# GpSimd subtractions and products of two tensors in pieces of at most 256 columns, in a two-layer streaming step

## The chip, the core and the metric

The kernel runs on one core of a Trainium2 chip. TensorE (PE in the profile) does the matmuls, VectorE (DVE), ScalarE (ACT) and GpSimd (POOL) work on tiles in SBUF and PSUM, each engine takes its instructions in the order in which they were written to its queue, and semaphores make one engine wait for another. What counts is device time in microseconds, the median over several executions.

## The reference

One step of a two-layer encoder for two request groups: a new stream of 2048 frames with 16 meta tokens ahead of it, and 8 running streams of 16 frames. Together these are 2192 rows of 1024 numbers, all in fp32. Each layer is a norm, one combined input projection, two groups of heads side by side, a gate, and an output projection:

```
layer 0:  u = rmsnorm(x);  p = u @ w_in
          s5_mixer: complex diagonal recurrence, associative_scan over time, gelu, GLU
          mlstm_mixer: xc = silu(causal_conv(x)); q, k = xc @ wq, xc @ wk; v = x @ wv
                       gates = [q k v] @ w_if; chunks of 64 carry (C, n, m)
                       y = head_norm(h) * norm_w + skip * xc
          out = (gated branches) @ w_out, added to x
layer 1:  the same frame with rope, retention (chunked state S), and
rglru_mixer:  xc = causal_conv(x);  r, i = sigmoid(xc @ w_a + b_a), sigmoid(xc @ w_x + b_x)
              a = exp(-8 * softplus(lam) * r);  h_t = a_t * h_(t-1) + sqrt(1 - a_t^2) * (i * xc)
```

The outputs are both groups' rows and every new state. There is no reduced precision: a product of two fp32 tensors is made of rounded halves, as told next.

## The kernel before

An fp32 tensor x that goes into a matmul is cut into two fp32r parts, h = round(x) and l = x - h, and a product is three matmuls (`mm3`, L111 to L113: h*h, l*h or h*l, so that in most places L113 reads the second operand's l and L112 the first one's). `split` (L103) makes the parts: ACT casts x to h at L105, and DVE or, with `pool=True`, GpSimd subtracts at L106. The profile names every split by its tiles: `wl` and `p_wl` are the low parts of weight tiles of 128x1024 (eight blocks of 128 columns), `p_xcl` that of a convolved tile of 128x384 or 128x272, `m_xcl` that of an mLSTM tile of 128x1024, `rol` and `r_gl` those of the last output projection, `p_wal` a 128x256 gate weight.

The stages in the order of time, with the profile's microseconds:

- 0 to 260, input norm and projection of the S5 half of layer 0 (`phase_in0`), weights split on DVE and GpSimd in turn.
- 260 to 900, the other columns of layer 0's projection (`phase_l0`, L341). For every weight tile, projections into `pm`, a causal convolution on DVE (`conv4`, L537 and L539) over `xb`, its split (ACT L389, GpSimd L391 into `xbl`), a SiLU on ACT (L408) and the gate matmuls `pg` (L414) that read its result. Beside it runs the S5 recurrence (`s5`, L676): on DVE a chain of five small instructions per time step (L764 to L768, 0.2 us each).
- 900 to 1230, the mLSTM (`phase_mlstm`, `ml_scores`, `ml_normed`, `ml_gated`), units of 128 rows. GpSimd makes `m_g` = xc * skip (L1161), one step of the normaliser `m_sm` (L1179, L1180), the mask (L1147) and the gate product `m_zb` = m_g * m_zb (L1199); DVE makes `m_qs` (L1131) and adds the normalised heads from PSUM to `m_g` (L1197), which frees the PSUM tile `pa` for the next unit's projection.
- 1230 to 1560, output projection of layer 0.
- 1560 to 2600, input projection of layer 1 (`phase_in1`, L1553). From 1675 it goes in eight periods of 79.2 us, one for each 128 columns of the RG-LRU, with six row blocks b = 0 to 5 each. For a block: PE projects into `p_pm`; ACT copies it to `p_x` (L1612); DVE convolves it into `p_xc` (L537, L539; block 5 also has the running streams, by way of `p_xd`, L1620); ACT casts `p_xch` (L105); GpSimd subtracts `p_xcl` (L106); PE multiplies by the gate weight into `p_pg` (L111 reads `p_xch`, L112 `p_xcl`); ACT and DVE run the gates and the scan (L1632 to L1662, `p_z` last).
- 2600 to 3150, retention and the last output projection (`phase_ret`), whose splits are `r_kl`, `r_pl`, `rol`, `r_gl`, and whose rope product `r_ld` is at L1786.

Tile pools give out buffers and put in the waits. The order within a queue is made by a scheduler that lists the instructions with estimated durations, so a change of some instructions can move others. The order is printed below where it matters.

Of the kernel before, what the change touches and what calls it, by code (L numbers as in the profile page):

```python
# [13 lines left out]
OP = mybir.AluOpType  # L14
# [9 lines left out]
KD = 8  # L24
# [78 lines left out]
def split(nc, h, l, x, pool=False, act=True):  # L103

    (nc.scalar.copy if act else nc.vector.tensor_copy)(h, x)  # L105
    (nc.gpsimd if pool else nc.vector).tensor_tensor(l, x, h, op=OP.subtract)  # L106


def mm3(nc, out, a, b, start, stop, **kw):
# [67 lines left out]
def norm_u(e, ps, x, n, rs, nwb, uh, ul, pname, pbufs, keep=None):  # L177


    nc = e.nc  # L180
    nc.vector.scalar_tensor_tensor(x[:n], x[:n], rs[:n], nwb[:n], op0=OP.mult, op1=OP.mult)
    for g in range(2):
        pt = ps.tile([128, 4, 128], F32, name=pname, bufs=pbufs)
        for j in range(4):
            k = 4 * g + j
            nc.tensor.transpose(pt[:, j, :n], x[:n, 128 * k:128 * (k + 1)], e.ident[:n, :n])
        sl = slice(4 * g, 4 * g + 4)
        split(nc, uh[:, sl, :], ul[:, sl, :], pt[:, :, :n])
        if keep:
            keep(sl, uh[:, sl, :], ul[:, sl, :])  # L190
# [12 lines left out]
def phase_in0(e):  # L203
# [6 lines left out]
    with P(e, "a_w") as wp, P(e, "a_sb", 2) as sb, PS(e, "a_ps") as ps:  # L210
# [37 lines left out]
        for i, bi in enumerate(seq):  # L248
# [8 lines left out]
            if i == 0:  # L257
                m0 = 4
                pms = [ps.tile([128, 384], F32, name="pm0", bufs=4) for _ in range(4)]
                for k in range(KD):  # L260
                    wr = st.tile([128, 1024], F32, name="a_st", bufs=A_ST)
                    nc.sync.dma_start(wr, w[:, k, 0:1024])
                    split(nc, wh[k], wl[k], wr, pool=k % 2 == 1)
                    for m in range(4):
                        mm(pms[m], m, k)
                for m in range(4):
                    out(m, pms[m], zst, b0, n)
# [14 lines left out]
            if i == 4:  # L282

                fp = opn(e, "w_first", side="right")
                wr = sb.tile([128, 1024], F32, name="xt", bufs=3).rearrange("p (k n) -> p k n", n=128)
                nc.sync.dma_start(wr, w[:, :, 1024:1152])
                e.wf = [fp.tile([128, KD, 128], F32R, name="wf" + x) for x in "hl"]
                split(nc, *e.wf, wr)
# [52 lines left out]
def phase_l0(e):  # L341

    nc, tc = e.nc, e.tc
# [12 lines left out]
    def mtile(third, m, isz, ut, pg, parts):  # L356

        h0 = ut[0][1]
        ncol = ut[1][1] + ut[1][2] - h0
# [12 lines left out]
        else:  # L372
            xb = xp.tile([128, 772], F32, name="xb1")
# [14 lines left out]
        xbh = xp.tile([128, 768], F32R, name="xbh1")  # L388
        nc.scalar.copy(xbh[:, :ncol], xb[:, 3:3 + ncol])  # L389
        xbl = xp.tile([128, 768], F32R, name="xbl1")  # L390
        nc.gpsimd.tensor_tensor(xbl[:, :ncol], xb[:, 3:3 + ncol], xbh[:, :ncol], op=OP.subtract)  # L391
        xc = sb.tile([128, 768], F32, name="xc1")
        if third == 0:
            nc.gpsimd.memset(xb[:, 0:3], 0.0)
# [63 lines left out]
    for third in range(3):  # L458
# [6 lines left out]
        if third > 0:  # L465

            early = [mtile(third, 0, 0, ut, pg, parts),
                     mtile(third, third % 2 == 0, third % 2, ut, pg, parts)]
            for g in early:
                next(g)  # L470
            reload(2 * third + 1)
            e.s5.loaded = third == 2
# [576 lines left out]
def ml_scores(e, sb, lp, hp, pt, slots):  # L1049


    nc, v = e.nc, e.nc.vector
    sk = e.row["ml_skip"]
    dec, meta = slots[0] == 0, slots[0] == 1
    n = NM if meta else 128
# [24 lines left out]
    if meta:  # L1080

        for g in range(2):
            pq = pt("pa", 2, 256)
            for j in range(2):
                for k in range(2):
                    c = 4 * g + 2 * j + k
# [8 lines left out]
    for g in range(0 if meta else 4):  # L1095
        pq = pt("pa", 2, N)
        for j in range(2):
            ms = slice(128 * j, 128 * (j + 1))
            for k in range(2):
                c = 2 * g + k  # L1100
# [6 lines left out]
        if dec:  # L1107
            pk = pt("pa", 2, N)
            for j in range(2):
                for k in range(2):  # L1110
                    c = 2 * g + k
# [4 lines left out]
    for i, slot in enumerate(slots):  # L1116
        r0, cc, cs = H * slot, c0 + n * i, slice(n * i, n * (i + 1))
        c = Env()
# [17 lines left out]
        for g in range(2):  # L1136
# [3 lines left out]
            for j in range(2):  # L1140
                h = 2 * g + j
# [16 lines left out]
        p = c.p = sb.tile([128, H, 128], F32, name="m_p", bufs=nb(2))  # L1158
        v.tensor_tensor(p[:n, :, :n], pS[:n, :, :n], w[:n, :, :n], op=OP.mult)
        g = c.g = sb.tile([128, KD, 128], F32, name="m_kt" if dec else "m_g", bufs=nb(2))  # L1160
        nc.gpsimd.tensor_tensor(g[:, :, :n], c.xc, e.pc[:, :, sk:sk + 1].to_broadcast([128, KD, n]), op=OP.mult)  # L1161
        res.append(c)
    return res

# [19 lines left out]
def ml_gated(e, c):  # L1184

    nc, v = e.nc, e.nc.vector
    nw, g, n = e.row["ml_norm_w"], c.g, c.n
    zb = c.sb.tile([128, KD, 128], F32, name="m_rw" if c.dec else "m_zb", bufs=1 if c.dec else 2)
    nc.sync.dma_start(zb[:, :, :n], e.zb[:, :, c.c0:c.c0 + n])
    for q in range(2):  # L1190
        py = c.pt("pa", 4, 128)
        for j in range(4):
            k = 4 * q + j
            nc.tensor.transpose(py[:, j, :n], c.yn[:n, k // 2, 128 * (k % 2):128 * (k % 2 + 1)], e.ident[:n, :n])
        for j in range(4):
            k = 4 * q + j
            v.scalar_tensor_tensor(g[:, k, :n], py[:, j, :n], e.pc[:, k, nw:nw + 1], g[:, k, :n],  # L1197
                                   op0=OP.mult, op1=OP.add)
    nc.gpsimd.tensor_tensor(zb[:, :, :n], g[:, :, :n], zb[:, :, :n], op=OP.mult)  # L1199
    nc.scalar.dma_start(e.gb[:, :, c.c0:c.c0 + n], zb[:, :, :n])  # L1200


def ml_running(e, sb, pt):


    nc, v, m = e.nc, e.nc.vector, e.m
    c, = ml_scores(e, sb, sb, sb, pt, [0])
    z = sb.tile([128, 2, NSEQ, 2 * LS], F32, name="m_z")
    nc.gpsimd.memset(z, 0.0)
# [846 lines left out]
```

## Time and profile before

| what | us |
|---|---|
| median of 3 runs | 3155.74 (3153.85 to 3159.35) |
| the profiled execution | 3151.14 |
| its span, first to last instruction | 3149.4 |
| PE busy | 3002.9 (95%), 17435 matmuls |
| DVE busy | 1728.6 (55%) |
| ACT busy | 1056.1 (34%) |
| GpSimd busy | 904.6 (29%), 931 instructions |

"Busy" is the time from an instruction's start to its end as the profiler records it, so an instruction that has started and cannot get at its data counts as busy. The mean granted clock of PE is 0.980. Between the first matmul and the last, PE stands still in some 77 gaps, about 130 us in all.

### The profile page before, as it was taken

To read this page: it belongs to the slowest core of one execution; us is meant where nothing else is said; L and a number is where in the kernel's file an instruction comes from. 1 tells how busy PE (TensorE), PEld (TensorE's weight loads), DVE (VectorE), ACT (ScalarE), POOL (GpSimd) and SP (SyncE) were. 2 spreads that over 40 slices of the span, in tenths; PEclk is the share of its full clock that TensorE was granted. 3 is DMA by queue.
4 is the path that set the end of the run, shared out by engine and by line. 5 is a ranking of instruction groups with operands and counts; after the bars stand their busy time and mean duration, and the time that the engine had idled before them with its cause. 6 is when DMAs were issued, how large, how long until landed. Compare 5 with 4: busy or idle time off the path is not lost.

```text
span 3149.4 us, 45106 instructions
## 1 busy us (share of the span) xinstructions
PE 3002.9 (95%) x17435; PEld 2717.0 (86%) x17435; DVE 1728.6 (55%) x3449; ACT 1056.1 (34%) x1858; POOL 904.6 (29%) x931
## 2 busy tenths in 40 slices
PE   8999978997999998999999999999999999999999
PEld 8999877996987887766799999999998897888887
DVE  4236798464447886243355667766620026665664
ACT  4223332335334443211224555555531112211211
POOL 6104424443225663111202111111110014433432
PEclk9999989998999999999999999999999999999999
DMA  6437433559454556755532111111122158444442
GB/s 213 117 82 206 125 117 113 159 166 177 141 159 125 157 156 183 232 185 172 158 132 73 51 51 50 49 50 49 49 81 75 55 151 251 140 119 133 136 124 74
DMA packets 444034, 396.36 MB, mean 126 GB/s; under 512 B 43401, under 2 KB 392785, under 8 KB 443818
## 3 DMA queue, kind: packets, MB, share of 16 engines
q1 hardware_dynamic: 333164, 268.13, 29.9%
q10 hardware_dynamic: 110654, 125.33, 12.0%
q8 instruction: 137, 2.24, 0.3%
q14 instruction: 79, 0.65, 0.1%
HBM read 262.12 MB, written 131.27 MB: 125 GB/s over the span
## 4 chain that ended last, share of the span: by engine, by line
PE 59%; DVE 8%; DMA 2%; issue 1%; ACT 1%; POOL 0%; SPq 0%; DVEq 0%; POOLq 0%; ACTq 0%
PE p_pm L112 8%; PE p_pm L113 8%; PE p_pm L111 8%; PE r_pm L112 4%; PE r_pm L113 4%; PE r_pm L111 4%; PE pa L111 3%; PE pa L112 3%; PE pa L113 3%; DVE p_d L1639 1%; PE pn L1288 1%; PE pc L1291 1%; DVE p_xc L537 1%; PE pa L1156 1%; DVE m_qs L1131 1%
## 5 line engine op out<-in xcount | busy, mean ns | idle before, releaser
L111 PE MATMUL p_pm<-pu,p_wh 128*128 128x384 f32 (+1 forms) x1568 | 512.2, 327 | 0.2 <-ACT pu L105 0.2
L112 PE MATMUL p_pm<-pu,p_wh 128*128 128x384 f32 (+1 forms) x1568 | 511.9, 327 | 0.0
L113 PE MATMUL p_pm<-pu,p_wl 128*128 128x384 f32 (+1 forms) x1568 | 511.3, 326 | 0.0
L111 PE MATMUL pm<-ub,wh 128*128 128x384 f32 (+1 forms) x1136 | 381.4, 336 | 3.4 <-ACT wh L105 2.9
L112 PE MATMUL pm<-ub,wh 128*128 128x384 f32 (+1 forms) x1136 | 380.1, 335 | 1.6 <-DVE ub L106 1.6
L113 PE MATMUL pm<-ub,wl 128*128 128x384 f32 (+1 forms) x1136 | 376.1, 334 | 0.0
L111 PEld LDWEIGHTS p_pm<-pu,p_wh 128*128 128x128 f32 x1568 | 294.2, 188 | 1.8 <-issue 1.2
L112 PEld LDWEIGHTS p_pm<-pu,p_wh 128*128 128x128 f32 x1568 | 294.6, 188 | 1.0 <-issue 0.8
L113 PEld LDWEIGHTS p_pm<-pu,p_wl 128*128 128x128 f32 x1568 | 294.5, 188 | 0.0
L111 PEld LDWEIGHTS pm<-ub,wh 128*128 128x128 f32 x1136 | 218.6, 193 | 9.0 <-issue 4.3
L112 PEld LDWEIGHTS pm<-ub,wh 128*128 128x128 f32 x1136 | 218.7, 193 | 3.0 <-DVE ub L106 2.1
L112 PE MATMUL r_pm<-rol,r_gh 128*128 128x512 f32 x544 | 217.6, 400 | 3.8 <-POOL rol L106 3.6
L113 PEld LDWEIGHTS pm<-ub,wl 128*128 128x128 f32 x1136 | 218.1, 192 | 1.2 <-issue 1.1
L111 PE MATMUL r_pm<-roh,r_gh 128*128 128x512 f32 x544 | 217.5, 400 | 0.9 <-ACT p_o L1549 0.9
L113 PE MATMUL r_pm<-roh,r_gl 128*128 128x512 f32 x544 | 216.9, 400 | 0.9 <-DVE r_gl L106 0.9
L106 POOL TENSOR_TENSOR p_wl<-p_wr,p_wh 128x1024 fp32r<-128x1024 f32 x34 | 81.8, 2407 | 385.3 <-ACT p_wh L105 372.9
L106 POOL TENSOR_TENSOR wl<-wr,wh 128x1024 fp32r<-128x1024 f32 x47 | 119.2, 2537 | 243.1 <-ACT wh L105 236.8
L112 PEld LDWEIGHTS r_pm<-rol,r_gh 128*128 128x128 f32 x544 | 102.7, 189 | 24.3 <-POOL rol L106 4.1
L113 PEld LDWEIGHTS r_pm<-roh,r_gl 128*128 128x128 f32 x544 | 102.8, 189 | 22.6 <-DVE r_gl L106 1.3
L111 PEld LDWEIGHTS r_pm<-roh,r_gh 128*128 128x128 f32 x544 | 102.3, 188 | 21.9 <-ACT p_o L1549 1.3
L106 POOL TENSOR_TENSOR p_xcl<-p_xc,p_xch 128x384 fp32r<-128x384 f32 (+1 forms) x48 | 46.8, 975 | 245.9 <-ACT p_xch L105 209.3
L1639 DVE RECIPROCAL p_d<-p_d 128x384 f32<-128x384 f32 (+1 forms) x48 | 116.7, 2430 | 0.6
(715 smaller groups left out, 6810.9 us busy)
## 6 DMA issues: line engine op xcount, KB each, us to landing
wr<-in_ev_w_in_dram SPq DMA_DIRECT2D x47, 512.0 KB
p_wr<-in_od_w_in_dram SPq DMA_DIRECT2D x40, 512.0 KB
d_in<-p_o ACTq DMA_DIRECT2D x80, 192.0 KB
m_rw<-d_grow SPq DMA_DIRECT2D x18, 512.0 KB
s5u<-d_ua SPq DMA_DIRECT2D x32, 274.0 KB
d_v<-vo ACTq DMA_DIRECT2D x68, 128.0 KB
m_va<-d_v SPq DMA_DIRECT2D x17, 512.0 KB
d_h<-o_x ACTq DMA_DIRECT2D x17, 512.0 KB
```

The lines of the kernel that those rows point to most:

```text
L106: (nc.gpsimd if pool else nc.vector).tensor_tensor(l, x, h, op=OP.subtract)
L111: nc.tensor.matmul(out, a[0], b[0], start=start, stop=False, **kw)
L112: nc.tensor.matmul(out, a[0], b[1], start=False, stop=False, **kw)
L113: nc.tensor.matmul(out, a[1], b[0], start=False, stop=stop, **kw)
L537: v.tensor_scalar(out, x(3), pc[:, m, cw + 3:cw + 4], pc[:, m, cb:cb + 1], op0=OP.mult, op1=OP.add)
L1131: v.tensor_tensor(qs[:, 4 * j:4 * j + 4, :n].rearrange("p (h m) n -> p h m n", m=2), qt[j][:, :, cs].rearrange("p (h m) n -> p h m n", m=2 ...
L1156: nc.tensor.matmul(pS[:n, h, :n], ktc[:, 2 * h + k, :], qt[h // 2][:, 2 * (h % 2) + k, cs], start=k == 0, stop=k == 1)
L1288: nc.tensor.matmul(pn[:n], c.qs[:, 2 * h + k, :n], ct[h][:, k, :], start=False, stop=k == 1)
L1291: nc.tensor.matmul(pc, c.kw[:n, h, 128 * k:128 * (k + 1)], c.va[:n, h, :], start=True, stop=True)
L1639: v.reciprocal(d[:, :n], d[:, :n])
```

## The change

A helper `narrow` issues a GpSimd `tensor_tensor` as several over slices of the first free dimension, such that none has more than 256 columns per partition. It takes the place of the single instruction in `split(pool=True)`, for `xbl`, for `m_g` (L1161) and for `m_zb` (L1199). All else is left: the rope product (L1786), the S5 products (L753, L818), and the splits on DVE. Line numbers after the helper grow by 12 (L111 becomes L123).

```diff
 def split(nc, h, l, x, pool=False, act=True):
     (nc.scalar.copy if act else nc.vector.tensor_copy)(h, x)
-    (nc.gpsimd if pool else nc.vector).tensor_tensor(l, x, h, op=OP.subtract)
+    if pool:
+        narrow(nc, l, x, h, OP.subtract)
+    else:
+        nc.vector.tensor_tensor(l, x, h, op=OP.subtract)
+
+def narrow(nc, out, a, b, op):
+    n = out.shape[1]
+    step = max(1, 256 * n // math.prod(out.shape[1:]))
+    for i in range(0, n, step):
+        c = slice(i, min(i + step, n))
+        nc.gpsimd.tensor_tensor(out[:, c], a[:, c], b[:, c], op=op)
...
-        nc.gpsimd.tensor_tensor(xbl[:, :ncol], xb[:, 3:3 + ncol], xbh[:, :ncol], op=OP.subtract)
+        narrow(nc, xbl[:, :ncol], xb[:, 3:3 + ncol], xbh[:, :ncol], OP.subtract)
...
-        nc.gpsimd.tensor_tensor(g[:, :, :n], c.xc, e.pc[:, :, sk:sk + 1].to_broadcast([128, KD, n]), op=OP.mult)
+        narrow(nc, g[:, :, :n], c.xc, e.pc[:, :, sk:sk + 1].to_broadcast([128, KD, n]), OP.mult)
...
-    nc.gpsimd.tensor_tensor(zb[:, :, :n], g[:, :, :n], zb[:, :, :n], op=OP.mult)
+    narrow(nc, zb[:, :, :n], g[:, :, :n], zb[:, :, :n], OP.mult)
```

The program's GpSimd instructions grow from 936 to 1589, those of the other engines stay the same but for three table loads of ACT fewer. The order moves too.

GpSimd in the mLSTM, around the gate product of one unit; before:

```order
L1199 TENSOR_TENSOR m_zb_10464<-m_g_9963,m_zb_10464 128x1024
L1147 AFFINE_SELECT m_w_10360<-m_w_10360 128x512
L1179 TENSOR_TENSOR m_sm_10805<-m_sm_10805,mhalf_84 128x1
L1161 TENSOR_TENSOR m_g_10335<-m_xc_10227,pc_549 128x1024
L1180 TENSOR_SCALAR m_sm_10805<-m_sm_10805 128x1
L1199 TENSOR_TENSOR m_zb_10571<-m_g_10005,m_zb_10571 128x1024
```

and the same unit after:

```order
L118 TENSOR_TENSOR m_zb_10391<-m_g_9866,m_zb_10391 128x256 x4
L1159 AFFINE_SELECT m_w_10284<-m_w_10284 128x512
L118 TENSOR_TENSOR m_g_10256<-m_xc_10142,pc_561 128x256 x4
L1191 TENSOR_TENSOR m_sm_10708<-m_sm_10708,mhalf_84 128x1
L118 TENSOR_TENSOR m_zb_10501<-m_g_9911,m_zb_10501 128x256
L1192 TENSOR_SCALAR m_sm_10708<-m_sm_10708 128x1
L118 TENSOR_TENSOR m_zb_10501<-m_g_9911,m_zb_10501 128x256 x3
```

One row has become four instructions, `m_g` goes ahead of a step of the normaliser, and such a step now stands between two pieces.

PE in `phase_in1`, where the first gate matmul of block 5 (`p_pg` from `p_xch`) stands in the next projection (`p_pm`, tile by tile of `pu`); before:

```order
L111 MATMUL p_pm_16174<-pu1_14739,p_wh_16142 128x384
L112 MATMUL p_pm_16174<-pu1_14739,p_wh_16142 128x384
L113 MATMUL p_pm_16174<-pu1_14739,p_wl_16143 128x384
L111 MATMUL p_pm_16174<-pu1_14739,p_wh_16142 128x384
L111 MATMUL p_pg_16081<-p_xch_16077,p_wah_15586 128x384
L112 MATMUL p_pm_16174<-pu1_14739,p_wh_16142 128x384
```

and after, ahead of these rows the first four matmuls of the same tile:

```order
L124 MATMUL p_pm_16596<-pu1_15146,p_wh_16561 128x384
L125 MATMUL p_pm_16596<-pu1_15146,p_wl_16562 128x384
L123 MATMUL p_pm_16596<-pu1_15146,p_wh_16561 128x384
L124 MATMUL p_pm_16596<-pu1_15146,p_wh_16561 128x384
L125 MATMUL p_pm_16596<-pu1_15146,p_wl_16562 128x384
L123 MATMUL p_pm_16596<-pu1_15146,p_wh_16561 128x384
L124 MATMUL p_pm_16596<-pu1_15146,p_wh_16561 128x384
L125 MATMUL p_pm_16596<-pu1_15146,p_wl_16562 128x384
L123 MATMUL p_pm_16596<-pu1_15146,p_wh_16561 128x384
L123 MATMUL p_pg_16500<-p_xch_16495,p_wah_15999 128x384
L123 MATMUL p_pg_16506<-p_xch_16495,p_wah_15999 128x384
```

The gate matmul stands nine matmuls of 128x384 later in that tile. DVE in the same place, from the end of block 4's scan to block 5's convolution; before:

```order
L1609 MEMSET p_x_17101 128x3
L1662 TENSOR_TENSOR p_z_16685<-p_z_16685,p_h_16658 128x384
L537 TENSOR_SCALAR p_xc_16806<-p_x_16803,pc_549 128x256
L1620 COPY p_xd_16811<-p_x_16803 128x8x16
L1622 COPY p_cs_14751<-p_x_16803 128x3
L539 SCALAR_TENSOR_TENSOR p_xc_16806<-p_x_16803,pc_549,p_xc_16806 128x256
L537 TENSOR_SCALAR p_xc_16806<-p_xd_16811,pc_549 128x128
```

and after:

```order
L549 TENSOR_SCALAR p_xc_17239<-p_x_17236,pc_561 128x256
L1632 COPY p_xd_17244<-p_x_17236 128x8x16
L1634 COPY p_cs_15158<-p_x_17236 128x3
L1674 TENSOR_TENSOR p_z_17117<-p_z_17117,p_h_17090 128x384
L551 SCALAR_TENSOR_TENSOR p_xc_17239<-p_x_17236,pc_561,p_xc_17239 128x256
L549 TENSOR_SCALAR p_xc_17239<-p_xd_17244,pc_561 128x128
```

The convolution now begins ahead of `p_z`.

## Rows read from the trace of the kernel before

**Rows 1.** The page's first part: engine, busy us (share of the span), instructions.

```profile
PE 3002.9 (95%) x17435; PEld 2717.0 (86%) x17435; DVE 1728.6 (55%) x3449; ACT 1056.1 (34%) x1858; POOL 904.6 (29%) x931
```

**Rows 2.** Waits of PE: what waited, for whom, total us, times, longest.

```profile
PE pg L414 <- ACT xc L408: 29.9, 9, 6.7
PE pa L111 <- DVE m_g L1197: 17.3, 5, 3.5
PE p_pg L111 <- ACT p_xch L105: 10.6, 8, 1.4
...
PE r_pm L112 <- POOL rol L106: 3.6, 1, 3.6
```

**Rows 3.** Groups by shape, POOL: busy us, mean ns, idle before and releasers.

```profile
L106 POOL TENSOR_TENSOR p_wl<-p_wr,p_wh 128x1024 fp32r<-128x1024 f32 x34 | 81.8, 2407 | 385.3 <-ACT p_wh L105 372.9 <-DMA p_wr<-in_od_w_in_dram 12.4
...
L106 POOL TENSOR_TENSOR p_wal<-p_wax,p_wah 128x256 fp32r<-128x256 f32 x8 | 5.9, 737 | 64.2 <-ACT p_wah L105 64.2
```

**Rows 4.** Timeline, DVE, S5 recurrence at 395: start, us, instruction.

```profile
395.70 2.42 DVE L768 TENSOR_TENSOR s5ee<-s5c,s5c 128x32 f32<-128x32 f32 x1
398.15 1.24 DVE L764 TENSOR_TENSOR s5c<-s5ee,s5a 64x32 f32<-64x32 f32 x1
399.41 0.21 DVE L765 TENSOR_TENSOR s5c<-s5ee,s5a 64x32 f32<-64x32 f32 x1
```

**Rows 5.** Timeline, POOL, the same stretch.

```profile
395.64 2.40 POOL L106 TENSOR_TENSOR wl<-wr,wh 128x1024 fp32r<-128x1024 f32 x1 [2.30 <-ACT wh L105]
398.00 1.35 POOL L391 TENSOR_TENSOR xbl<-xb,xbh 128x656 fp32r<-128x656 f32 x1
```

**Rows 6.** Timeline, all engines, the mLSTM unit at 1164.

```profile
1164.12 2.35 POOL L1199 TENSOR_TENSOR m_zb<-m_g,m_zb 128x1024 f32<-128x1024 f32 x1 [3.01 <-DMA m_rw<-d_grow]
...
1164.35 3.71 DVE L1131 TENSOR_TENSOR m_qs<-m_qt,m_rw 128x512 f32<-128x512 f32 x2
...
1166.43 1.09 POOL L1147 TENSOR_SCALAR_AFFINE_SELECT m_w<-m_w 128x512 f32<-128x512 f32 x1
...
1168.11 1.11 DVE L1197 SCALAR_TENSOR_TENSOR m_g<-pa,pc,m_g 128x128 f32<-128x128 f32 x4
...
1169.28 0.58 PE L111 MATMUL pa<-m_xch,amh 128*128 128x256 f32 x1 [3.46 <-DVE m_g L1197]
```

**Rows 7.** Timeline, DVE: another `m_qs` pair, then a period of `phase_in1`.

```profile
1184.96 1.29 DVE L1131 TENSOR_TENSOR m_qs<-m_qt,m_rw 128x512 f32<-128x512 f32 x2 [1.83 <-DMA m_rw<-d_grow]
...
1796.25 0.49 DVE L1662 TENSOR_TENSOR p_z<-p_z,p_h 128x384 f32<-128x384 f32 x1
...
1800.49 2.58 DVE L1662 TENSOR_TENSOR p_z<-p_z,p_h 128x384 f32<-128x384 f32 x1
...
1804.62 2.53 DVE L537 TENSOR_SCALAR p_xc<-p_xd,pc 128x128 f32<-128x128 f32 x1
...
1808.21 0.72 DVE L539 SCALAR_TENSOR_TENSOR p_xc<-p_xd,pc,p_xc 128x128 f32<-128x128 f32 x2
```

**Rows 8.** Timeline, POOL, the same period.

```profile
1800.26 2.39 POOL L106 TENSOR_TENSOR p_wl<-p_wr,p_wh 128x1024 fp32r<-128x1024 f32 x1 [13.72 <-ACT p_wh L105]
1802.91 1.03 POOL L106 TENSOR_TENSOR p_xcl<-p_xc,p_xch 128x384 fp32r<-128x384 f32 x1 [0.26 <-ACT p_xch L105]
1804.65 2.41 POOL L106 TENSOR_TENSOR p_wl<-p_wr,p_wh 128x1024 fp32r<-128x1024 f32 x1 [0.71 <-ACT p_wh L105]
```

**Rows 9.** Timeline, ACT and PE, the same period.

```profile
1801.88 0.48 ACT L1612 COPY p_x<-p_pm 128x384 f32<-128x384 f32 x1
...
1809.58 0.44 PE L111 MATMUL p_pg<-p_xch,p_wah 128*128 128x384 f32 x1 [1.40 <-ACT p_xch L105]
```

**Rows 10.** Timeline, DVE and POOL, the convolution at 360 in `phase_l0`.

```profile
358.90 3.33 POOL L106 TENSOR_TENSOR wl<-wr,wh 128x1024 fp32r<-128x1024 f32 x1
...
359.94 2.98 DVE L539 SCALAR_TENSOR_TENSOR xc<-xb,pc,xc 128x656 f32<-128x656 f32 x1
```

**Rows 11.** Timeline, POOL, the retention stage at 2669, behind the rope product.

```profile
2669.82 2.34 POOL L106 TENSOR_TENSOR rol<-r_yn,roh 128x1024 fp32r<-128x1024 f32 x1
```

## The prediction

> **What bounds the kernel now.** The page first: PE is busy 95% of the span, DVE 55%, POOL 29% [rows 1]. GpSimd has some 2245 us in which nothing runs, so its own busy time sets no bound. PE's gaps come to about 130 us, and nothing off PE can give back more than that. So the second view is who PE waits for [rows 2]. Two large entries name DVE as the last link: the gate matmuls `pg`, which wait for ACT's SiLU, itself fed by DVE's convolution (29.9 us), and the mLSTM projection `pa`, held by DVE's `m_g` (17.3 us in five waits). A third, `p_pg` (10.6 us in eight), waits for ACT's cast of what DVE convolved. Only 3.6 us name POOL.
>
> The third view is DVE beside POOL. In the S5 recurrence a DVE instruction of 32 columns lasts 0.21 us. The one that starts at 395.70, just after GpSimd's `wl` split (395.64, 2.40 long), lasts 2.42, to 398.12; the next, under `xbl` (398.00, 1.35), lasts 1.24 and ends at 399.39 [rows 4, 5]. A DVE instruction with its data in SBUF stands still until the GpSimd instruction that runs has ended; then DVE gets one instruction in, and the next GpSimd instruction blocks it again. It repeats: `p_z` lasts 2.58 at 1800.49 under `p_wl` and 0.49 at 1796.25 alone; one `p_xc` of 128 columns lasts 2.53 under the next `p_wl` [rows 7, 8]; two `m_qs` take 3.71 under `m_zb` and the mask, and 1.29 without [rows 6, 7]. The price also runs the other way: `wl` at 358.90 takes 3.33, nearly 1 us above its usual length [rows 10].
>
> The Trainium skill ("SBUF — State Buffer", "Who interferes with whom") says the same: VectorE's second port pair is GpSimd's, and it is an exclusive lock for a whole instruction. The durations just named agree.
>
> So the question is whether a lock held for about 0.65 us, four times, costs the path of PE's gaps less than one held for 2.4.
>
> **The change part by part.** GpSimd's own time: a 128x256 subtraction takes 0.737 us, one of 1024 columns 2.407 [rows 3]. Four are 2.948, so 0.541 more, or 180 ns for each instruction added. 653 more instructions make up to 118 us of POOL time, less some 40 ns each for the overlap that two instructions in a row show (395.64 + 2.40 against 398.00): 91 to 118 us. Off the path this costs nothing: the weight splits run a projection tile ahead of their use, and POOL idles over twice a microsecond for each one added. If that cover were gone, PE would wait for `wl`, `p_xcl` or `rol`; that is a rival below. A piece's data part is 0.737 - 0.180 = 0.56.
>
> Where a single DVE instruction meets a long split, it waits for one piece instead of the whole:
>
> - The convolution at 360: L539 of 656 columns lasts 2.98, about 0.9 of it work. With GpSimd's pieces of 0.65 to 0.74 its wait falls from about 2.1 to 0.7: **-1.35** in a PE gap of 3.38 that waits for `pg`. The same gap of the second pass, at 673, has 3.11 us and a similar chain: **-1**. Bounds together 0 (the following convolution steps meet the pieces left over) to -3.
> - The mLSTM: five gaps of 3.46 us, alike. In the last, `m_zb` runs from 1164.12, the mask behind it, and the two `m_qs` between end at about 1168.0; `m_g` follows at 1168.11 and PE at 1169.28 [rows 6]. After the change the queue there still has `m_zb`, then the mask. The first `m_qs` waits for one piece (to about 1164.8) and ends at 1165.35, the second for the next piece (to 1165.95) and ends at 1166.5, L1178 for the third; `m_g` begins at about 1167.2 instead of 1168.1. That is -0.9 each, **-4.5**. Bounds: 0, if the pieces hold DVE as long as before, to five times -1.3. The normaliser step that now stands behind `m_g`'s four pieces comes 2 us later; its reader on ACT ran at 1172.7, with PE's transposes of it a unit behind, so that is cover enough.
> - `phase_in1`, eight gaps of 1.40 at `p_pg` of block 5 [rows 2, 9]. Two things change. DVE: the convolution starts ahead of `p_z`, and ACT's copy `p_x` no longer stands behind a table load, so that it follows the weight cast at once (`p_wl`, which waits for that cast, starts at 1800.26 [rows 8]) and is there at about 1800.7 instead of 1802.36 [rows 9]. The chain (two L537, six L539, three copies and `p_z`, about 3.9 us of work) now lies under two `p_wl` of eight pieces: four from 1800.2, four from 1804.65, when the second cast has come. Nearly every one of its instructions waits for a piece: 1800.7 + 3.9 + about 4.3 = 1808.9, the same end as before (1808.93, [rows 7]). DVE as such gains nothing here. PE: the gate matmul stands nine matmuls of 0.174 us later, 1.57 us that used to be gap and now is work. 1.40 - 1.57 is below nothing, so about 1.2 of each gap goes: **-9** over eight. Bounds: -11 (all) to +3 (the chain 0.7 later than PE's new arrival plus the 1.40). Block 4 comes to its gate matmul 1 us earlier, but its convolution is done by 1799 and the matmul is due at about 1802.7.
> - The retention gap of 3.64 us [rows 2]: `rol` starts at 2669.82 behind the rope product and takes 2.34 [rows 11]; PE reads it block by block, so it can go on after the first pieces: **-0.9**, bounds 0 and -1.6.
>
> Where DVE is dense with small instructions (S5 recurrence, 380 to 510), the lock alternates: seven pieces in place of `wl` and `xbl` block seven instructions for a short time instead of two for a long one. Before, DVE lost 2.42 + 1.24 - 2 x 0.22 = 3.2 us [rows 4]. After, the data parts hold it just as long (3.2), and the five fixed parts of 180 ns hold it fully or not at all: 3.2 to 4.1. Some 38 added instructions in that stretch make 0 to +7 us on DVE. The chain that ends `pg`'s 23 us of gaps there runs over DVE, but most of its convolution steps meet no split. I take **0**, with -2 to +7.
>
> The rest is order: the stretch 900 to 1230 and the gaps at 745 to 785, which an ACT instruction behind a DMA sets, come in another order on all engines. I see no sign to give them: **0**, with 6 either way.
>
> Sum: -2.3 - 4.5 - 9 - 0.9 = -16.7 us. The profiled execution took 3151.1, 4.6 below the median of the runs, so 3134 in a profile and **3139 us** as a median, -0.5%. Shorter gaps may also spare some stretches at the lower granted clock that follow the long ones; I count nothing for it.
>
> **Rivals.**
> *The alternation takes it all back (no change).* If after each piece DVE gets exactly one instruction, every dense chain loses what it lost. Then the mLSTM and convolution terms fall to about nothing and the dense stretch pays +4, while PE's reorder in `phase_in1` gives half: about 3155. For it speak the two blocked instructions in a row at 395.70 and 398.15; against it that the mLSTM's pair is only two instructions long.
>
> *The fixed part decides (slower).* Each piece costs DVE its whole 0.737, not 0.56: +7 in the S5 stretch; in `phase_in1` eight pieces add 8 x 0.18 = 1.4 to the chain, which gives the 1.2 back; in the mLSTM units 12 pieces for `m_zb`, `m_g` and `m_xcl` add some 9 x 0.18 = 1.6 each, in about eight units before their gap ends, 8 to 13 us. Sum about +10 to +18: 3168. It decides if DVE loses over 0.65 us for each piece it meets. The Trainium skill ("GPSIMD Engine Reference", section 3.1 and the dispatch figures beside it) has a fixed cost for each GpSimd instruction, which speaks for such a price; the 180 ns above are this kernel's.
>
> *POOL comes late (slower).* Between two pieces DVE takes its turn, so a four-piece split lasts up to 4 x (0.74 + 0.5) = 5 us beside a dense DVE. `p_xcl` in two pieces ends some 0.4 us later; the time between PE's L111 and L112 that hides it is 1.04 us where it is least, and `p_xcl` alone takes 1.03 [rows 8]. If PE waits 0.5 us at each of the 48, that is +24 against -17: 3163.
>
> *More is won.* If `pg`'s gaps of 5 to 7 us also shrink by a piece's difference, and lower-clock stretches go with them: another -12, 3127.
>
> **How the numbers follow.** Forecast as summed 0.50, more won 0.13, alternation 0.20, the two slower ones 0.17 together. A measurement of this kernel can tell 0.2% (6.3 us) from no change: faster, below 3149.4, takes the first two and a little of the third: 0.66. Same, to 3162: 0.19. Slower 0.15. The range reaches from "more won" with its reorder bound (3121) to the slower cases' lower part (3162); the forecast's own range is 3129 to 3149.
>
> **What would show it.** In the profile after: a 128x256 row of `wl` at about 0.65 to 0.74 us and POOL at about 1000 us busy; no DVE row of 2.4 us under a split, but runs of several at 0.6 to 0.8; PE's five waits for `m_g` at about 2.6 us; the eight waits for `p_xch` gone or below 0.3; no wait of PE for POOL's `p_xcl`. I am wrong if the S5 stretch's `pg` waits grow by more than a few us, or if new waits come up in the mLSTM.

## The result and the profile after

The change makes the kernel slower: median 3169.48 us (3165.16 to 3172.07, five runs) against 3153.85 (3149.38 to 3159.35, five runs) for the kernel before, a ratio of 1.0054 with the interval [1.0041, 1.0068]. The forecast, 3139, had the wrong sign, and the time lies 7.5 us above the range.

The page's first part of the changed kernel (engine, busy us, share of the span, instructions; span 3167.8 us), against [rows 1]:

```profile
PE 3013.3 (95%) x17435; PEld 2719.1 (86%) x17435; DVE 1663.7 (53%) x3449; ACT 1051.8 (33%) x1855; POOL 1093.3 (35%) x1584
```

DVE is 65 us less busy: as meant, it stands less behind GpSimd. Yet PE is 10.4 us busier with the same matmuls (10.3 of it in the retention stage, where the mean granted clock is 0.97 instead of 0.99), and it stands still longer by the rest of the 18.4 us that the span has grown. To see where, the span is cut at the same six matmuls in both traces. The busy time by stage (window, its length, then busy us and instructions of PE, PEld, DVE, ACT, POOL, then PE's granted clock, DMA share, GB/s), kernel before:

```profile
0.00:913.00 913.00, 827.77 (x5369) 793.23 (x5369) 515.79 (x918) 321.28 (x605) 324.25 (x292) 0.96 0.53 149
913.00:1220.00 307.00, 275.35 (x1608) 239.12 (x1609) 241.44 (x716) 127.47 (x269) 172.48 (x208) 0.93 0.48 144
...
1682.00:2287.00 605.00, 594.38 (x3570) 591.83 (x3569) 425.81 (x709) 323.62 (x495) 103.82 (x76) 1.00 0.15 48
...
2643.00:3149.00 506.00, 493.35 (x2481) 411.66 (x2479) 305.59 (x621) 101.51 (x158) 192.04 (x184) 0.99 0.45 129
```

The same stages of the changed kernel:

```profile
0.00:907.00 907.00, 823.16 (x5369) 788.04 (x5369) 488.67 (x918) 320.43 (x603) 414.42 (x539) 0.97 0.52 150
907.00:1230.00 323.00, 279.51 (x1614) 237.21 (x1615) 215.93 (x724) 125.89 (x271) 192.12 (x344) 0.94 0.46 138
...
1693.00:2284.00 591.00, 591.00 (x3562) 591.00 (x3561) 428.26 (x707) 323.76 (x491) 138.52 (x188) 1.00 0.15 50
...
2644.00:3168.00 524.00, 503.61 (x2483) 418.71 (x2481) 297.08 (x624) 101.04 (x158) 223.32 (x277) 0.97 0.44 125
```

Two stages gain: everything up to 913 us by 6, and `phase_in1` by 14, where PE now never stops (591.00 of 591.00). Two lose more: the mLSTM (907 to 1230) takes 16 us longer, though DVE is 25.5 us less busy there, and the retention stage 18. PE's idle time grows from 31.7 to 43.5 us in the mLSTM and from 12.7 to 20.4 in the retention stage.

Who PE waits for (what waited, for whom, total us, times, longest), the answer to [rows 2]:

```profile
PE pg L426 <- ACT xc L420: 27.0, 10, 5.9
PE pn L1298 <- ACT m_yn L1193: 15.1, 5, 5.5
PE pc L1303 <- DVE ct L1307: 14.8, 8, 4.9
...
PE pa L1206 <- ACT m_yn L1193: 6.5, 4, 3.4
PE r_pm L125 <- DVE r_gl L109: 6.0, 2, 4.2
...
PE r_pm L123 <- ACT roh L105: 3.1, 1, 3.1
PE pa L123 <- DVE m_g L1209: 3.0, 2, 1.5
...
PE r_pm L124 <- POOL rol L118: 0.9, 3, 0.5
```

What was to shrink has shrunk: `pa` for `m_g` from 17.3 to 3.0, `rol` from 3.6 to 0.9, `p_pg` for `p_xch` from 10.6 to no entry at all. But `pn` and `pa` for ACT's `m_yn`, `pc` for `ct` (4.4 us in the mLSTM before) and `r_pm` for `r_gl` and `roh` are new or much larger.

GpSimd's groups by shape (busy us, mean ns, idle before), against [rows 3]:

```profile
L118 POOL TENSOR_TENSOR wl<-wr,wh 128x256 fp32r<-128x256 f32 x188 | 179.1, 983 | 180.0 <-ACT wh L105 179.8
L118 POOL TENSOR_TENSOR p_wl<-p_wr,p_wh 128x256 fp32r<-128x256 f32 x128 | 103.3, 838 | 253.2 <-ACT p_wh L105 253.2
```

On the mean a piece of these splits lasts 0.84 to 0.98 us, not the 0.737 of [rows 3]. The mean hides two kinds (shortest, median and longest in ns):

```profile
L118 POOL TENSOR_TENSOR wl<-wr,wh x188: 719/741/2615, 255.0 to 892.7; 128x256 fp32r<-128x256 f32 x188
```

Half of the pieces take 0.741 us or less, beside the small DVE instructions of S5 too (four in 2.82 us, below); each of the 51 that take over 1 us overlaps a DVE instruction of 512 columns or more (convolutions, S5 products). The stretch of S5 that [rows 4, 5] showed, on DVE and then on GpSimd (start, us, instruction):

```profile
390.30 0.73 DVE L777 TENSOR_TENSOR s5c<-s5ee,s5a 64x32 f32<-64x32 f32 x1
391.06 0.67 DVE L778 TENSOR_TENSOR s5c<-s5ee,s5a 128x32 f32<-128x32 f32 x1
391.65 0.80 DVE L779 TENSOR_TENSOR s5c<-s5c,s5ee 128x32 f32<-128x32 f32 x1
392.48 0.66 DVE L780 TENSOR_TENSOR s5ee<-s5c,s5c 128x32 f32<-128x32 f32 x1
393.18 0.54 DVE L776 TENSOR_TENSOR s5c<-s5ee,s5a 64x32 f32<-64x32 f32 x1
393.73 0.58 DVE L777 TENSOR_TENSOR s5c<-s5ee,s5a 64x32 f32<-64x32 f32 x1
```

```profile
390.24 2.82 POOL L118 TENSOR_TENSOR wl<-wr,wh 128x256 fp32r<-128x256 f32 x4 [3.77 <-ACT wh L105]
393.03 1.63 POOL L118 TENSOR_TENSOR xbl<-xb,xbh 128x256 fp32r<-128x256 f32 x3
```

One DVE instruction passes per piece (one more, not shown, runs under the end of the seventh and last piece, in 0.37 us). The six come to 3.98 us where 6 x 0.22 = 1.32 would do: 2.7 lost, against the 3.2 of before. The Trainium skill ("SBUF — State Buffer", "Who interferes with whom") calls the shared port pair an exclusive lock; the trace agrees, with 0.54 to 0.80 us for each of the six instructions shown.

### The profile page after: what moved, and what is told of

It reads as the page before. It is cut to its first block, busy times and chain, and to the rows that moved or that the text cites. A ratio compares the mean times of both kernels' runs of the same rounds, so it can differ in the third digit from the quotient of the medians.

```text
span 3167.8 us, 45858 instructions
## 1 busy us (share of the span) xinstructions
PE 3013.3 (95%) x17435; PEld 2719.1 (86%) x17435; DVE 1663.7 (53%) x3449; ACT 1051.8 (33%) x1855; POOL 1093.3 (35%) x1584
## 4 chain that ended last, share of the span: by engine, by line
PE 77%; DMA 8%; DVE 8%; POOL 3%; issue 2%; ACT 1%; ACTq 1%; SPq 0%; DVEq 0%; POOLq 0%
PE p_pm L125 10%; PE p_pm L124 10%; PE p_pm L123 10%; PE r_pm L125 4%; PE r_pm L124 4%; PE r_pm L123 4%; PE pm L123 4%; PE pm L124 4%; PE pm L125 4%; PE pa L123 3%; PE pa L124 3%; PE pa L125 3%; DMA m_rw<-d_grow 2%; DVE xc L551 1%; PE pn L1300 1%
## 5 line engine op out<-in xcount | busy, mean ns | idle before, releaser
L123 PE MATMUL p_pm<-pu,p_wh 128*128 128x384 f32 (+1 forms) x1568 | 512.5, 327 | 0.2 <-ACT pu L105 0.2
L123 PE MATMUL pm<-ub,wh 128*128 128x384 f32 (+1 forms) x1136 | 380.3, 336 | 10.0 <-ACT vo L451 8.8
L123 PEld LDWEIGHTS p_pm<-pu,p_wh 128*128 128x128 f32 x1568 | 294.5, 188 | 1.4 <-issue 0.8
L118 POOL TENSOR_TENSOR wl<-wr,wh 128x256 fp32r<-128x256 f32 x188 | 179.1, 983 | 180.0 <-ACT wh L105 179.8
L123 PEld LDWEIGHTS pm<-ub,wh 128*128 128x128 f32 x1136 | 217.4, 192 | 15.0 <-ACT vo L451 9.4
L123 PE MATMUL r_pm<-roh,r_gh 128*128 128x512 f32 x544 | 220.0, 405 | 3.3 <-ACT roh L105 3.1
L118 POOL TENSOR_TENSOR p_wl<-p_wr,p_wh 128x256 fp32r<-128x256 f32 x132 | 108.4, 852 | 262.0 <-ACT p_wh L105 262.0
L118 POOL TENSOR_TENSOR p_xcl<-p_xc,p_xch 128x256 fp32r<-128x256 f32 x96 | 61.4, 660 | 319.6 <-ACT p_xch L105 284.4
L123 PEld LDWEIGHTS r_pm<-roh,r_gh 128*128 128x128 f32 x544 | 104.4, 192 | 25.2 <-ACT roh L105 3.3
```

Of the source, the lines that this page charges most:

```text
L118: nc.gpsimd.tensor_tensor(out[:, c], a[:, c], b[:, c], op=op)
L123: nc.tensor.matmul(out, a[0], b[0], start=start, stop=False, **kw)
```

## The experiments

**Theories.** *Order* (mine, after seeing the traces): the pieces do what the forecast says, but with 653 more instructions the scheduler lists all queues in another order, and that order is worse in the mLSTM and the retention stage. *Pieces*: their fixed cost and the alternation with DVE are the loss. To part them, the order of a queue has to be set apart from the pieces. An order table does it: every instruction is tied to the one that is to stand ahead of it on its queue, by an edge that fixes the order and adds no semaphore. The table itself costs nothing that can be seen: e9 below holds the change's own order by one, and its time isn't told apart from the change's.

```diff
+def pinned(tc):
...
+        for p, q in zip(row, row[1:]):
+            tc.add_manual_dep(own[q], own[p].name, dep, reason="order")
...
+        pinned(tc)
```

In e1 the changed kernel has the order of before on all queues (the pieces where the whole stood). In e2 the kernel before has the order of after (a whole instruction where its last piece stands).

> The changed kernel's pieces, with every engine's queue in the order of the kernel before (a piece stands where its whole instruction stood). Theory 'order': the loss of the change (+19 us in the retention stage, +12 in the mLSTM, by the time between the same matmuls in the two traces) comes from the new order, and the pieces themselves help: some 3140 to 3150 us, ratio 0.995 to 0.999, with the five waits for m_g at about 2.6 us and no wait of PE for m_yn. The eight waits of p_pg stay near 1.4 to 1.6 us, since their gain was PE's order. Theory 'pieces': what is lost is DVE and GpSimd time under the lock, so the loss stays without the new order: 3163 us or more, ratio 1.003 or more.

> Whole GpSimd instructions as before, with every engine's queue in the order of the changed kernel (a whole instruction stands where its last piece stood). Theory 'order': as slow as the changed kernel or slower, 3165 to 3180 us, ratio 1.004 to 1.009, with the long waits for m_yn in the mLSTM. Theory 'pieces': no loss, 3145 to 3157 us, ratio 0.997 to 1.001, with the eight waits of p_pg shorter.

| | whole | pieces of 256 |
|---|---|---|
| order of before | 1 | e1: 0.9954 [0.9938, 0.9969], 3134.75 us |
| order of after | e2: 1.0143 [1.0128, 1.0159], 3195.25 us | 1.0054 [1.0041, 1.0068] |

The pieces gain in either order, 0.5% in the old and 0.9% in the new one. The order costs 1.4% with whole instructions and 1.0% with pieces. So *pieces* falls as the cause of the loss; e2's loss is even larger than *order* expected (1.009 at most). The waits of PE in e1:

```profile
PE pg L428 <- ACT xc L422: 22.5, 10, 4.7
PE pa L1170 <- DVE m_p L1173: 10.7, 6, 2.2
...
PE p_pg L125 <- ACT p_xch L107: 9.8, 7, 1.4
...
PE pa L125 <- DVE m_g L1211: 7.8, 5, 1.8
```

The five waits for `m_g` fall from 3.46 to 1.6 us each, and those for `p_xch` stay, as the forecast's steps say. But six waits for `m_p`, 10.7 us, are new, and in the mLSTM they take the place of what `m_g` gives back. The stage's window in e1:

```profile
908.00:1206.00 298.00, 266.98 (x1607) 230.37 (x1608) 230.89 (x721) 127.94 (x271) 200.16 (x342) 0.97 0.50 149
```

PE stands still for 31.0 us there, against 31.7 before. What the stage gains is PE's busy time, 275.35 to 266.98, with a granted clock of 0.97 instead of 0.93: the gaps are shorter and more, and by these means PE spends some 18 us at the lower of its clock levels instead of 43.

**Where.** The difference to the trace of before by stage, between the same matmuls (us; one execution each, whose time lies up to 6 us from the median of its kernel, e13's 6.0 below it; a stage with the same queues and instructions differs by up to 5 us between two executions, as e4 with -3.4 and e5 with +1.7 do up to 913; mLSTM to the last `pn` from `ct`, then to the first `p_pg`, the last `p_pg`, the last `p_pm`, the end):

| | to 913 | mLSTM | to 1682 | in1 | to 2643 | retention | all |
|---|---|---|---|---|---|---|---|
| after | -5.8 | +15.6 | +1.7 | -14.4 | +3.7 | +17.5 | +18.3 |
| e1 pieces, old order | -4.5 | -9.2 | +1.7 | -1.1 | +0.5 | +0.4 | -12.2 |
| e2 whole, new order | +0.1 | +31.6 | -1.5 | -6.5 | +1.3 | +18.2 | +43.2 |
| e8 mixed order | -10.8 | -7.7 | +2.3 | -12.6 | +2.2 | +1.0 | -25.6 |
| e10 old load queue | -2.5 | +1.0 | +20.3 | -14.0 | +8.0 | +17.6 | +30.4 |
| e13 the same, to mLSTM's end | -11.7 | +4.0 | +1.5 | -14.4 | +1.7 | +17.0 | -1.9 |

The retention stage loses about the same with whole instructions (+18.2) as with pieces (+17.5): nothing but order is left there. In `phase_in1` order and pieces share the gain: the eight waits come to 10.6 before, 9.8 with pieces alone, 5.7 with the order alone, and none with both.

**One stage at a time, scheduler free.** The step becomes the whole tile outside the named stages.

```diff
-    step = max(1, 256 * n // math.prod(out.shape[1:]))
+    step = max(1, 256 * n // math.prod(out.shape[1:])) if STAGE[0] in PIECES else n
...
+PIECES = ('phase_in0', 'phase_l0', 'phase_in1')
```

e4 has `('phase_mlstm',)` there and e5 `('phase_ret',)`.

> Pieces in the two input projections (phase_in0, phase_l0, phase_in1) alone, whole instructions elsewhere; the scheduler then leaves the queues of the mLSTM, the output projection and the retention stage as they were before. By the time between the same matmuls in the two traces these stages gave -12 (to 760 us), +6 (760 to 900) and -13 (1680 to 2360). Theory 'order' and theory 'pieces' both: 3132 to 3140 us, ratio 0.993 to 0.996, if the loss of the other stages is their own; near 3154 if it was passed on from the earlier stages.

> Pieces in the mLSTM (phase_mlstm) alone; other stages' queues as before. If the mLSTM's own new order makes its loss: +8 to +18 us, 3162 to 3172, ratio 1.003 to 1.006, with PE waiting for m_yn. If the loss there came from what the earlier stages shifted: -4.5 us as I summed, ratio 0.998 to 1.000.

> Pieces in the retention stage (phase_ret) alone, whole instructions elsewhere; the other stages' queues as before, the stage's own queues as the scheduler then makes them. If the loss of 19 us there is that stage's own new order: 10 to 20 us slower than before, ratio 1.003 to 1.006. If it was passed on from the stages ahead, as the mLSTM's loss was (pieces there alone cost nothing, ratio 1.0008): ratio 0.999 to 1.001.

e3: 0.9969 [0.9956, 0.9982]. Part of its expectation did not hold: the mLSTM's queues were not those of before. They came in another order although no instruction of that stage was cut, and the stage lost 12 us, with `pc` waiting for `ct` (8.6 us, 4.4 before). Of SP's queue only one load changed its place in that stage, so the order of the other engines can cost that much without it. e4: 1.0008 [0.9997, 1.0020], no difference; the mLSTM's own pieces, with the order that the scheduler makes for them, cost nothing that can be told (3 us in the stage). e5: 1.0018 [1.0007, 1.0028], with 9 us lost in the retention stage. So an edit in one stage sets the order of stages behind it, and a stage alone doesn't show what it does together with others.

**What in the mLSTM's order.** The changed kernel at 1099 to 1112: DMA issues (SP's queue), then GpSimd, ACT and PE.

```profile
1099.34 1.24 SPq L1201 DMA_DIRECT2D m_zb<-d_zb  x2
1100.66 1.02 SPq L1140 DMA_DIRECT2D m_va<-d_v  x1
1101.78 2.12 SPq L1134 DMA_DIRECT2D m_rw<-d_grow  x1
```

```profile
1105.91 0.27 POOL L1192 TENSOR_SCALAR m_sm<-m_sm 128x1 f32<-128x1 f32 x1
```

```profile
1109.49 1.28 ACT L1158 ACTIVATE m_w<-m_rw,acol 128x128 f32<-128x128 f32 x4 [6.61 <-DMA m_rw<-d_grow]
1110.67 1.00 ACT L1193 ACTIVATE m_yn<-pn,m_sm 128x256 f32<-128x256 f32 x2
```

```profile
1111.27 1.23 PE L1298 MATMUL pn<-m_va,m_p 128*128 128x258 f32 x2 [5.49 <-ACT m_yn L1193]
```

The load of `m_rw` (the rows of gate values from which `m_w` and `m_qs` are made) is issued behind two loads of `m_zb` and one of `m_va`. ACT waits 6.61 us for it with `m_w`; `m_yn`, whose scale `m_sm` GpSimd had ready at 1106.2, stands behind `m_w` in ACT's queue; PE waits for `m_yn`. The other three waits of `pn` for `m_yn` over 2 us (at 999.7, 1039.6 and 1207.3) have the same chain ahead of them. SP issued nothing from 1092.90 to 1099.34: the loads of `m_zb` stood first, and DVE read the old content of an `m_zb` tile until 1099.31:

```profile
1097.15 2.16 DVE L109 TENSOR_TENSOR wol<-m_zb,woh 128x1024 fp32r<-128x1024 f32 x1 [1.66 <-ACT woh L105]
```

In the kernel before `m_rw` went ahead of `m_zb`, and on ACT `m_yn` ahead of `m_w`; its issues and ACT in the like place:

```profile
1104.44 0.78 SPq L1122 DMA_DIRECT2D m_rw<-d_grow  x1
1107.04 1.24 SPq L1189 DMA_DIRECT2D m_zb<-d_zb  x2
```

```profile
1109.11 0.56 ACT L1181 ACTIVATE m_yn<-pn,m_sm 128x256 f32<-128x256 f32 x1 [0.48 <-POOL m_sm L1180]
1111.77 1.28 ACT L1146 ACTIVATE m_w<-m_rw,acol 128x128 f32<-128x128 f32 x4 [2.10 <-DMA m_rw<-d_grow]
```

Three runs ask whether the load's place does it. All have the pieces and the order of after, but: e9 a third buffer for `m_rw`, e10 SP's queue (the loads) as before throughout, e13 SP's queue as before up to the mLSTM's end.

```diff
-        rw = c.rw = lp.tile([128, 2, H, 128], F32, name="m_rw", bufs=nb(2))
+        rw = c.rw = lp.tile([128, 2, H, 128], F32, name="m_rw", bufs=nb(3))
...
```

(The same number changes at the two other tiles of that name.)

> The changed kernel (pieces of 256, its own order held fixed on every queue) with three buffers instead of two for the mLSTM's row-weight tile m_rw. In the changed kernel ACT waits 47.0 us for m_rw's DMA in the mLSTM (19.7 before), and the normaliser's output m_yn stands behind it on ACT's queue. Theory 'the new order reads m_rw to its end later, so that the next load starts late': ACT's wait falls to 25 us or less and the mLSTM's loss of 12 us goes to a half or more: 3153 to 3162 us where the changed kernel has 3165 to 3169, ratio 1.000 to 1.003. Theory 'the load is late for its place on SP's queue, or something else': no difference, ratio 1.004 to 1.007.

> The changed kernel with SP's queue (the DMA issues) alone in the order of the kernel before, all other queues in the new order. If the place of the loads on SP's queue makes the loss in the mLSTM or the retention stage: ratio 1.002 or less. If it is the compute queues' order: ratio 1.004 to 1.008.

> The changed kernel, its own order held fixed, with SP's queue in the order of the kernel before up to the end of the mLSTM and in the new order from there. In the changed kernel the load of m_rw is issued behind two loads of m_zb and one of m_xc (1101.78 for a use that starts at 1109.49), before it stood ahead of them. Theory 'SP's place of the loads': the 14 us that SP's old queue gave back in the mLSTM stay, and the loss that it opened in the output projection does not come: 3150 to 3158 us, ratio 1.000 to 1.003. Theory 'the compute queues' order': as the changed kernel, 1.004 to 1.007.

e9: 1.0046 [1.0029, 1.0063], not told apart from the change itself, and ACT still waits 42.9 us for `m_rw`; a third buffer alone doesn't help. e10: 1.0078 [1.0059, 1.0098], slower, but by its stages (table) the mLSTM gives back 15 us, and 19 are lost behind it, where PE waits for loads that the old queue has late for the new order:

```profile
PE pn L1252 <- DMA m_c<-in_state_ml_c_dram: 12.4, 5, 5.3
```

e13 (its expectation says `m_xc` where the rows show `m_va`) leaves that loss out: 1.0005 [0.9994, 1.0016], 15 us better than the change. Its mLSTM takes 4.0 us more than before instead of 15.6, and by its end it is 17.5 us ahead of after. ACT's waits for `m_rw` at `m_w` between 900 and 1240 us, in before, after and e13:

```profile
ACT m_w L1146 <- DMA m_rw<-d_grow: 19.7, 15, 3.7
```

```profile
ACT m_w L1158 <- DMA m_rw<-d_grow: 47.0, 15, 6.6
```

```profile
ACT m_w L1160 <- DMA m_rw<-d_grow: 31.6, 12, 4.4
```

PE's wait of `pn` for `m_yn` halves with it, from 15.1 to 7.4. So the place of the loads is shown as the larger part of the stage's 15.6 us, and as about half of the 24.8 us that lie between e1 and the change. That it is the load of `m_rw` among them is argued from the chain above; e13 moves all loads. What remains, the 4.0 and the 9.2 that e1 gains, goes with the order of the other engines: `pc` still waits 12.9 us for `ct` in e13 (14.8 in after, 2.4 in e1). No run put ACT's or DVE's queue back alone, so which of them it is stays open.

**What in the retention stage.** PE's windows over its first 77 us, before and after:

```profile
2643.00:2720.00 77.00, 71.15 (x355) 57.61 (x354) 54.24 (x91) 22.73 (x31) 39.76 (x31) 0.98 0.60 173
```

```profile
2644.00:2721.00 77.00, 66.42 (x296) 52.18 (x295) 42.27 (x72) 17.95 (x23) 49.10 (x47) 0.87 0.53 154
```

and what PE waited for in after:

```profile
2649.88 0.79 PE L125 MATMUL r_pm<-roh,r_gl 128*128 128x512 f32 x1 [4.22 <-DVE r_gl L109]
...
2686.41 1.22 PE L123 MATMUL r_pm<-roh,r_gh 128*128 128x512 f32 x2 [3.06 <-ACT roh L105]
```

PE idles 4.7 us more (10.6 against 5.9). Around these two waits, and twice more, it runs at the lower of its two clock levels (1.2 of 2.4 GHz) for a while: a mean of 0.87 over 77 us is some 20 us at half speed, where 0.98 was 3. Half of the 17 more, 8.5 us, is work lost. Together that makes 13 of the 17.5. A wait of 1.95 us for GpSimd's `r_kl` at 2767.4, with a mean clock of 0.91 over the 20 us around it, makes most of the rest. Then one queue at a time was put back to the old order in this stage alone: GpSimd's (e14), PE's (e15), SP's (e16).

> Pieces in the retention stage alone, with the order that the scheduler then makes there (11 us of loss in the trace, 1.0018 by the times), but GpSimd's queue in the order of before. If GpSimd's order (r_kl and rol against the rope product and r_sm) makes the loss: the stage at 0 to +3 us, ratio 0.999 to 1.001. Otherwise +8 to +12 us, 1.002 to 1.004.

> As the run before, but PE's queue in the order of before and all others as the scheduler makes them. If PE's order makes the loss (r_pm's parts ahead of what feeds them): 0 to +3 us in the stage, ratio 0.999 to 1.001. Otherwise +8 to +15 us.

> As the two runs before, but SP's queue (the loads) in the order of before. If the loads' places make the loss, as in the mLSTM: 0 to +3 us in the stage, ratio 0.999 to 1.001. Otherwise +8 to +12 us, as with SP's old queue in the whole program, which gave nothing back there.

1.0101 [1.0082, 1.0120], 1.0065 [1.0048, 1.0082] and 1.0049 [1.0031, 1.0067]: all three are slower than e5, from which they differ by that one queue. Its stage loses 9 us, theirs 25, 16 and 12; e14's is more than either branch of its expectation. So putting one queue back gives nothing back. A queue in one order among others in another makes waits of its own (in e14, `r_o` for GpSimd's `r_pl`, 8.0 us; in e15, `r_pm` for `rol`, 9.6). That order is the cause of the 17 us follows from e1 and e2; which queue's order stays open.

**The size of a piece.** The change's `256` becomes another number, in the old order (e6 512, e7 128) or with the scheduler free (e11 512).

```diff
-    step = max(1, 256 * n // math.prod(out.shape[1:]))
+    step = max(1, 512 * n // math.prod(out.shape[1:]))
```

> Pieces of at most 512 columns instead of 256, in the order of the kernel before. If what is won (0.9954 with 256) comes from a shorter wait of DVE for the instruction that runs, half the pieces win half to two thirds of it: a wait of at most 1.2 to 1.3 us, ratio 0.996 to 0.998. If it comes from something that the first cut gives at once (PE reading the first part early): 0.995.

> Pieces of at most 128 columns, in the order of the kernel before: 1500 GpSimd instructions more than whole ones. Theory of the wait: waits of 0.4 us, a little more won where a single DVE instruction meets a split; theory of the fixed part of a piece (180 ns): it holds DVE longer in dense places and GpSimd's splits end later. The two about cancel: ratio 0.994 to 0.998; above 0.998 the fixed part decides at this size.

> Pieces of at most 512 columns, the order left to the scheduler. Held to the old order, 512 gave 0.9933 and 256 gave 0.9954, and with 256 the free order cost 1.0 percent over the held one. If any new order costs about as much: ratio 1.001 to 1.005. If the loss is a matter of which order happens to come out: anything from 0.990 to 1.005, and the two are not tied.

| old order | ratio | DVE busy | GpSimd busy |
|---|---|---|---|
| whole | 1 | 1728.6 | 904.6 |
| e6, 512 | 0.9933 [0.9918, 0.9947] | 1689.0 | 964.3 |
| e1, 256 | 0.9954 [0.9938, 0.9969] | 1661.9 | 1077.8 |
| e7, 128 | 0.9984 [0.9974, 0.9994] | 1621.7 | 1250.7 |

DVE's busy time falls with every halving; the kernel's doesn't follow it. 512 and 256 aren't told apart, and 512 gains more than either theory of e6 allowed (0.995 at best); 128 is worse than both by the medians. The one execution of e7 that was traced is 6 us faster than its median and doesn't show why: it gains 16.4 us up to 913 and 9.2 in `phase_in1`, and its mLSTM takes 9.7 more than before where that of 256 takes 9.2 less. With the scheduler free 512 gives 1.0035 [1.0022, 1.0047], slower again, by yet another order.

**A better version.** e8 has pieces of 256, the new order up to about 735 us and in `phase_in1`, and the old one elsewhere; e12 is the same with 512.

> Pieces of 256 everywhere; the queues in the new order up to about 735 us and in phase_in1, in the order of before between and after. If the gains of the stages add: -12 us to 735 (instead of -8.6), some -6 to -7 in the mLSTM, -11 to -13 in phase_in1 where PE's order is the new one, +1 in the retention stage: -26 to -31 us, ratio 0.990 to 0.992. If the gain before 735 is lost again on the way, as in the run with pieces in the projections alone: ratio 0.993 to 0.995.

> Pieces of 512 in the mixed order of the best run so far (new up to 735 us and in phase_in1, old elsewhere; 0.9906 with 256). Held to the old order 512 stood 7 us ahead in the mLSTM and 4 us behind in phase_l0: ratio 0.988 to 0.991. If the mixed order's gains need the shorter pieces (phase_in1's gate matmuls wait for a chain under two p_wl): 0.991 to 0.994.

e8: 0.9906 [0.9887, 0.9924], 3122.08 us, faster than both kernels. Its page:

```profile
PE 2996.4 (96%) x17435; PEld 2708.9 (87%) x17435; DVE 1675.7 (54%) x3449; ACT 1053.5 (34%) x1855; POOL 1088.2 (35%) x1584
```

GpSimd is as busy as in the changed kernel; PE is busy 17 us less and stands still less. By the table it keeps the gains at both places and loses neither 16 nor 18. e12: 0.9967 [0.9954, 0.9980], worse than both of its theories: the eight waits for `p_xch` come to 12.8 us (1.2 in e8), and `phase_in1` takes 4 us more than before, not 12.6 less. The new order there needs the short pieces.

## Why the prediction was wrong

The step that failed is the term for order: "I see no sign to give them: **0**, with 6 either way". It was the largest term of all: e1 against the change puts it at 1.0%, some 31 us. It was given for the stretch 900 to 1230 and the gaps at 745 to 785; that the retention stage could lose by its order (+17.5) wasn't considered. The comparison of the two orders was to be had beforehand, and in it `m_rw` had gone behind `m_zb` on SP and `m_w` ahead of `m_yn` on ACT. The prediction looked at PE, DVE and GpSimd where they touched its own terms; SP's and ACT's queues in the mLSTM weren't followed to their readers, and "I see no sign" was taken for no effect. Of the prediction's own signs of being wrong the second one came: new waits in the mLSTM.

The terms of the sum, one by one:

- *Convolution, -2.3, and S5, 0.* Up to 913 us the change gains 5.8, the pieces alone 4.5. The sign is right, the size about double, but the parts are others: the gap at 363.8 goes from 3.38 to 0.76 us, twice the 1.35; the 3.11 of the second pass comes back as two of 1.49 and 1.61; the four long `pg` waits of S5, put at 0, go from 21.3 to 17.4 (14.1 in e1); two new ones, 4.3 together, come up at 277 and 287. In all PE idles 83.8 instead of 85.2 us there, and 4.6 of the 5.8 are its busy time (827.77 to 823.16), which the forecast left at nothing. In S5 the lock alternates as costed; it takes 2.7 us for a pair of splits, a little below the 3.2 to 4.1.
- *mLSTM, -4.5.* The step from pieces to shorter waits for `m_g` was right and undersized: 1.6 us a wait where 2.6 were forecast. That the stage gains by it was not: the waits for `m_p` take their place, and of the 9.2 us that e1 gains 8.4 are PE's busy time, by the clock. For that the prediction says "I count nothing for it". In the new order it is buried under +25.
- *"that is cover enough"* for the normaliser step behind `m_g`: GpSimd's step did come in time (1106.2), but `m_yn` behind it was late for another reason, its place behind `m_w`. At 1224.9 GpSimd did come late: `m_yn` waited 8.3 us for its `m_sm` and PE 3.35 for `m_yn`. The cover was sought at the producer and not in the reader's own queue.
- *`phase_in1`, -9.* The eight waits are gone, and the stage gains 14.4. PE's reorder alone takes only half of the waits (5.7 left of 10.6); that DVE gains nothing from pieces holds in the old order (9.8 left), not in the new. At 128 columns 1.7 us in seven waits are left even in the old order.
- *Retention, -0.9.* The wait for `rol` went from 3.6 to 0.9, as forecast; the stage's +17.5 has to do with other waits.
- *GpSimd's time, +91 to +118.* It grew by 189, because many pieces beside a wide DVE instruction last longer than 0.74 us, up to 2.6. It cost little directly: PE's waits for `wl` come to 2.9 us, the one at 1224.9 to 3.35, and none is for `p_xcl`.

Of the rivals, the fixed part came to 3168, nearly the time measured, but not by its mechanism: its condition (DVE loses over 0.65 us for each piece it meets) isn't met in S5, where the loss is 2.7 us in six, 0.45 each, and e1 with the same pieces is 0.5% faster. GpSimd coming late is excluded as the main cause by the waits just named. That the alternation takes all back is excluded by e1. That e1's 3134.75 lies in the forecast's own range, 3129 to 3149, is luck: 9 of the forecast's 16.7 us came from PE's new order in `phase_in1`, which e1 doesn't have, and the 7.7 that are left are half of the 14.6 that e1 gains. (The lower end of the stated range is off too: "more won" with the reorder's bound gives 3125, not 3121.)

## What to carry to other kernels

Where a scheduler sets the order, an edit that changes the number of instructions is two changes: test the edit in the old order and the old work in the new order before judging it. Read the new order on every queue, the DMA queue and the queue of the reader included, and follow each load that has moved behind others to the engine that waits for it. A helping engine's instructions are worth cutting where another engine waits once or twice behind a long one. How short depends on the order: in the old one 512 and 256 columns gained and 128 gained less, in e8's order 256 gained nearly three times what 512 did. And where a gap shrinks, look whether another takes its place, and what the clock makes of it.

## What was not expected of the hardware

- A GpSimd subtraction of 128x256 took 0.74 us also beside a dense row of small DVE instructions, and up to 2.6 us beside wide ones (`wl`, mean 0.98): the waiting goes both ways.
- Under a row of pieces one DVE instruction ran for each, with 0.54 to 0.80 us instead of 0.21.
- In the mLSTM of e1 PE stood still as long as before (31.0 and 31.7 us), in shorter gaps, and was busy 8.4 us less, at a granted clock of 0.97 instead of 0.93.
- At the head of the retention stage PE stood still 4.7 us more, and with that came some 17 us more at the lower clock, by the granted clock worth about 8.5 us, more than the gaps themselves.
